# Block products by Strassen's scheme in place of direct 2x2 products, in the dense stages behind attention

## The chip, the cores and the metric

The kernel runs on one core of one Trainium2 chip. The metric is device time in microseconds of the whole program. The engines are TensorE (PE, with its weight loads PEld), VectorE (DVE), ScalarE (ACT), GpSimd (POOL) and SyncE (SP), which issues nearly all DMAs.

## The reference

One layer of a trunk, sequence 1024, width 1024, 16 heads of 64, MLP width 4096, float32. Cut to what matters:

```python
h = rms_norm(x, norm1_g)
q, k, v, bg, cg, xc = split(h @ w_in)                       # six times 1024 columns
y_attn = chunked_relpos_attention(q, k, v, ...)             # band of 9 chunks of 64
u = cg * xc
conv = conv_b + sum(conv_w[j] * pad(u)[:, j:j + s] for j in range(3))
y_attn = y_attn @ w_attn_proj
y_conv = (bg * conv) @ w_conv_proj
g_attn, g_conv = split(sigmoid(h @ w_gate + b_gate))        # 2048 columns
x = x + (g_attn * y_attn + g_conv * y_conv) @ w_out
h2 = rms_norm(x, norm2_g)
u = square(relu(h2 @ w_up))                                 # 4096 columns
x = x + u @ w_down
```

## The kernel before

Activations lie transposed, features on the 128 partitions and the 1024 positions along the row, in two halves `c` of 512. Every dense product has float32 operands that are split in two numbers: `split` has ScalarE copy the value to the short type fp32r (`hi`, L83) and VectorE subtract (`lo`, L84). A product of one tile of 128 inner rows (a k-tile) is then three matmuls, hi x hi, lo x hi and hi x lo, of a 128x128 weight block on 512 columns, added up in one PSUM bank. `fetch_w` loads a weight tile by DMA (`r_...`), `split_w` splits it (`w_...`). `matmul` issues through `pin`, which ties each matmul to the one before it; so TensorE's order is the order of the code. The order of the other engines is a scheduler's; each engine runs its own in order.

The program has these stages. (1) Attention, one pair of heads after the other, with the next pair's projection woven in; in the last pair's place the first NG = 5 row tiles of the gates are woven in. (2) The gates' row tiles 5 to 15: `gate_stages` and `t_stages`, 48 matmuls a row tile (two halves, eight k-tiles, three matmuls), result to DRAM in `gD`. (3) The conv branch: for each of eight row tiles the products c, x and b, the taps on VectorE, the result split into `yc`. (4) The projection of the conv branch (cp), of attention (ap), each times its gate, then the output projection (out), each eight row tiles of 48 matmuls by `t_layout`. The mean square of the residual comes from `mean_square`, two matmuls, a tensor_scalar and a reciprocal for each half. (5) The MLP in 16 steps: `up(k)` makes 256 rows of the hidden layer, `down(k)` adds their products to `acc` in SBUF, with up one step ahead of down. An evacuation of a PSUM bank (the `ev` functions) is one or more VectorE operations for each half.

```python
                for n, (i, j) in enumerate(((0, 0), (1, 0), (0, 1))):
                    matmul(st[c][:], w[:, i, kt % 4, :], mov[c][:, j, kt, :],
                           kt == 0 and n == 0, kt == ND - 1 and n == 2)
```

The whole of the code that the change touches:

Of the kernel before, what the change touches and what calls it, by code (L numbers as in the profile page):

```python
# [40 lines left out]
def block_kernel(ctx, tc, x, xt, wqkv, wcnv, wgate, wcp, wap, wout, wup, wdown,  # L41
# [105 lines left out]
    def t_layout(*a):  # L147
        load, halves = t_stages(*a)
        load()
        for h in halves:  # L150
            for f in h:
                f()

    def new_act(name):
        return [apool.tile([P, 2, ND, HC], F32R, name=f"{name}{c}", tag="act") for c in range(2)]


    hT = new_act("hT")
# [406 lines left out]
    wpool = ctx.enter_context(tc.tile_pool(name="wpool", bufs=2, side="right"))  # L565
    psx = ctx.enter_context(tc.tile_pool(name="psx", bufs=6, space=PSUM))
    banks = [(psx, "x")] * 3 + [(psmm, "mm")] + [(psx, "x")] * 3 + [(psmm, "mm")]
    for t in range(NG, 16):
        if t == NG + 2:
            wp = (wpool, 7, 2)  # L570
        for f in gate_stages(t):
            f()
    att.close()
    acc = [[None] * 2 for _ in range(ND)]

    with tc.tile_pool(name="bpool", bufs=2) as bpool:

        yc = [bpool.tile([P, 2, ND, HC], F32R, name=f"yc{c}", tag="b") for c in range(2)]
        with tc.tile_pool(name="cv", bufs=1) as cv:
            rb2 = cv.tile([P, S], F32, name="rb2")  # L580
            nc.vector.tensor_tensor(rb2[:], rb[:], rb[:], op=ALU.mult)
            for t in range(ND):
                cs = cv.tile([P, S], F32, name=f"cs{t}", tag="cs")
                u = cv.tile([P, S + 2], F32, name=f"u{t}", tag="u")
                y = cv.tile([P, S], F32, name=f"y{t}", tag="y")

                def ev_c(c, ps):
                    cc = slice(c * HC, (c + 1) * HC)
                    nc.vector.tensor_tensor(cs[:, cc], ps[:], rb2[:, cc], op=ALU.mult)

                def ev_x(c, ps):
                    nc.vector.tensor_tensor(u[:, 2 + c * HC:2 + (c + 1) * HC], ps[:],
                                            cs[:, c * HC:(c + 1) * HC], op=ALU.mult)

                def ev_b(c, ps):
                    yy = y[:, c * HC:(c + 1) * HC]
                    nc.vector.tensor_tensor(yy, ps[:], yy, op=ALU.mult)
                    split(yc[c][:, 0, t, :], yc[c][:, 1, t, :], yy)

                t_layout(wcnv[1, t], hT, ev_c, f"c{t}")  # L600
                nc.gpsimd.memset(u[:, 0:2], 0.0)
                t_layout(wcnv[2, t], hT, ev_x, f"x{t}")
                cw = [sv[:, C_CW + 8 * j + t:C_CW + 8 * j + t + 1] for j in range(3)]
                nc.vector.tensor_scalar(y[:], u[:, 2:], cw[2], sv[:, C_CB + t:C_CB + t + 1],
                                        op0=ALU.mult, op1=ALU.add)
                for j in (1, 0):
                    nc.vector.scalar_tensor_tensor(y[:], u[:, j:j + S], cw[j], y[:],
                                                   op0=ALU.mult, op1=ALU.add)
                nc.vector.tensor_tensor(y[:], y[:], rb[:], op=ALU.mult)
                t_layout(wcnv[0, t], hT, ev_b, f"b{t}")  # L610


        aoT = new_act("aoT")
        with tc.tile_pool(name="mg", bufs=2) as mg:
            for p in range(NH // 2):
                for c in range(2):
                    a = mg.tile([P, HC], F32, name=f"a{p}_{c}", tag="a")
                    nc.sync.dma_start(a[:], aoD[p][c][:])
                    split(aoT[c][:, 0, p, :], aoT[c][:, 1, p, :], a[:])

            def gate_of(t, c):
                g = mg.tile([P, HC], F32, name=f"gl{t}_{c}", tag="gl")
                nc.sync.dma_start(g[:], gD[t][:, c * HC:(c + 1) * HC])
                nc.scalar.activation(g[:], g[:], AF.Sigmoid, bias=sv[:, C_BG + t:C_BG + t + 1])
                return g


            for t in range(ND):
                def ev(c, ps, t=t):
                    g = gate_of(ND + t, c)  # L630
                    nc.vector.tensor_tensor(g[:], ps[:], g[:], op=ALU.mult)
                    nc.sync.dma_start(mcD[t][:, c * HC:(c + 1) * HC], g[:])
                t_layout(wcp[t], yc, ev, f"cp{t}")


            mT = [bpool.tile([P, 2, ND, HC], F32R, name=f"mT{c}", tag="b") for c in range(2)]
            for t in range(ND):
                def ev(c, ps, t=t):
                    g = gate_of(t, c)
                    mc = mg.tile([P, HC], F32, name=f"mc{t}_{c}", tag="mc")  # L640
                    nc.sync.dma_start(mc[:], mcD[t][:, c * HC:(c + 1) * HC])
                    nc.vector.tensor_tensor(g[:], ps[:], g[:], op=ALU.mult)
                    nc.vector.tensor_tensor(g[:], g[:], mc[:], op=ALU.add)
                    split(mT[c][:, 0, t, :], mT[c][:, 1, t, :], g[:])
                t_layout(wap[t], aoT, ev, f"ap{t}")


        h2T = new_act("h2T")
        apl = ctx.enter_context(tc.tile_pool(name="apl", bufs=1, side="right"))
        rb2 = rb  # L650
        ssq = [apl.tile([P, HC], F32, name=f"ssq{c}") for c in range(2)]
        for t in range(ND):
            def ev(c, ps, t=t):
                a = acc[t][c] = apl.tile([P, HC], F32, name=f"acc{t}_{c}")
                nc.sync.dma_start(a.rearrange("p (s q) -> p s q", s=4),
                                    xt[4 * c:4 * c + 4, :, t, :].rearrange("s p q -> p s q"))
                nc.vector.tensor_tensor(a[:], ps[:], a[:], op=ALU.add)
                g2 = sv[:, C_G2 + t:C_G2 + t + 1]
                hi = h2T[c][:, 0, t, :]
                nc.scalar.activation(hi, a[:], AF.Copy, scale=g2)  # L660
                nc.vector.scalar_tensor_tensor(h2T[c][:, 1, t, :], a[:], g2, hi.bitcast(F32),
                                               op0=ALU.mult, op1=ALU.subtract)
# [120 lines left out]
```

## Time and profile before

| | us |
|---|---|
| median of 3 runs (1910.21 to 1910.93) | 1910.83 |
| the profiled execution, its own time | 1911.13 |
| its span, first to last instruction | 1909.3 |
| VectorE busy | 1058.8 (55%) |
| ScalarE busy | 560.7 (29%) |
| GpSimd busy | 164.0 (9%) |
| DMA queue 1, share of 16 engines | 28.7% |

The span is what the profile covers; the execution's own time is 1.8 us more. Busy shares are averages over stages. GpSimd's work lies almost all in attention; DMA moves 71 GB/s of HBM traffic on average.

### The profile page before, as it was taken

What the parts mean: (1) busy time and instruction counts of PE and PEld (TensorE: products, weight loads), DVE (VectorE), ACT (ScalarE), POOL (GpSimd) and SP (SyncE); (2) the same over time, 40 slices, a digit from 0 to 9 for tenths busy, and PEclk for the clock granted to TensorE, in tenths of its full rate; (3) what the DMA queues carried; (4) which work ended last, traced back from release to release, by engine and by line L of the source; (5) the groups of instructions that cost most, each with busy time, mean ns of one, the idle gap of its engine ahead of it and who ended that gap; (6) DMA issues with size and microseconds to landing.
All of it is one profiled execution on the core that took longest, in us unless ns stands there. A gap on an engine that the chain in (4) does not pass through costs nothing.

```text
span 1909.3 us, 24631 instructions
## 1 busy us (share of the span) xinstructions
PE 1882.7 (99%) x9268; PEld 1614.8 (85%) x9268; DVE 1058.8 (55%) x1966; ACT 560.7 (29%) x1117; POOL 164.0 (9%) x467
## 2 busy tenths in 40 slices
PE   6899999999999999999999999999999999999999
PEld 6899999999888888888888888888888888888887
DVE  6677877787642234435433445655555555555555
ACT  5455555555431111111232333211111111111110
POOL 5433233233000000000000000000000000000000
PEclk9999999999999999999999999999999999999999
DMA  6443443443322211111364451111111111111112
GB/s 245 111 109 92 104 110 92 111 110 88 111 86 96 94 56 50 50 45 51 109 215 143 144 156 54 36 53 50 50 45 49 52 45 50 50 45 44 50 51 93
DMA packets 91031, 162.08 MB, mean 85 GB/s; under 512 B 10912, under 2 KB 19104, under 8 KB 90912
## 3 DMA queue, kind: packets, MB, share of 16 engines
q1 hardware_dynamic: 90768, 160.48, 28.7%
q8 instruction: 73, 1.20, 0.3%
q14 instruction: 46, 0.38, 0.1%
q10 hardware_dynamic: 144, 0.03, 0.0%
HBM read 114.33 MB, written 20.97 MB: 71 GB/s over the span
## 4 chain that ended last, share of the span: by engine, by line
PE 95%; POOL 2%; DMA 1%; DVE 1%; ACT 1%; issue 0%; SPq 0%; DVEq 0%; POOLq 0%; ACTq 0%
PE ps_u L76 18%; PE pd L76 18%; PE psq L76 12%; PE ps_g L76 9%; PE ps_x L76 5%; PE ps_cp L76 5%; PE ps_o L76 5%; PE ps_ap L76 5%; PE ps_b L76 5%; PE ps_c L76 5%; PE av L76 3%; PE s L76 3%; PE tp L79 3%; POOL qw L115 0%; PE tq L79 0%
## 5 line engine op out<-in xcount | busy, mean ns | idle before, releaser
L76 PE MATMUL psq<-w_q,hT 128*128 128x384 f32 x1536 | 347.9, 352 | 11.2 <-ACT w_q L83 7.6
L76 PE MATMUL ps_u<-h2T,w_u 128*128 128x512 f32 x1536 | 355.2, 392 | 0.0
L76 PE MATMUL pd<-ut,w_d 128*128 128x512 f32 x1536 | 354.0, 391 | 0.0
L76 PEld LDWEIGHTS ps_u<-h2T,w_u 128*128 128x128 f32 x1536 | 288.5, 188 | 63.9 <-issue 1.0
L76 PEld LDWEIGHTS pd<-ut,w_d 128*128 128x128 f32 x1536 | 288.4, 188 | 63.1
L76 PEld LDWEIGHTS psq<-w_q,hT 128*128 128x128 f32 x1536 | 261.7, 193 | 15.2 <-ACT w_q L83 7.6
L719 DVE TENSOR_TENSOR acc<-pd,acc 128x512 f32<-128x512 f32 x256 | 176.5, 690 | 109.9 <-PE pd L76 107.7
L76 PE MATMUL ps_g<-hT,w_g 128*128 128x512 f32 x768 | 187.9, 395 | 0.0
L76 PEld LDWEIGHTS ps_g<-hT,w_g 128*128 128x128 f32 x768 | 140.6, 188 | 27.2
L689 DVE SCALAR_TENSOR_TENSOR rq<-ps_u,rb 128x512 f32<-128x512 f32 x64 | 44.2, 691 | 135.6 <-PE ps_u L76 135.5
L364 ACT ACTIVATE p<-p,sm 128x640 f32<-128x640 f32 (+4 forms) x128 | 89.7, 701 | 80.9 <-DVE sm L362 80.7
L83 ACT CAST ut<-rq 128x512 fp32r<-128x512 f32 x64 | 39.8, 622 | 216.1 <-DVE rq L691 216.1
L83 ACT CAST w_u<-r_u 128x512 fp32r<-128x512 f32 x64 | 39.9, 624 | 185.3 <-PE pd L76 107.7
L362 DVE CUSTOM_DVE_ANT_0 p<-s,b 128x640 f32<-128x640 f32 (+4 forms) x128 | 83.4, 652 | 12.8 <-PE s L76 9.6
L84 DVE TENSOR_TENSOR pt<-tp,pt 128x512 fp32r<-128x512 f32 (+1 forms) x144 | 84.2, 597 | 11.0 <-ACT pt L83 10.4
L76 PE MATMUL ps_x<-hT,w_x 128*128 128x512 f32 x384 | 89.2, 391 | 0.0
L76 PE MATMUL ps_c<-hT,w_c 128*128 128x512 f32 x384 | 89.2, 391 | 0.0
L76 PE MATMUL ps_b<-hT,w_b 128*128 128x512 f32 x384 | 89.2, 391 | 0.0
L76 PE MATMUL s<-k,q 128*128 128x384 f32 (+3 forms) x384 | 82.0, 322 | 6.4 <-DVE sm L362 6.2
L76 PEld LDWEIGHTS av<-pt,vt 128*128 128x128 f32 x576 | 85.5, 188 | 3.1 <-DVE pt L84 1.2
L83 ACT CAST w_d<-r_d 128x512 fp32r<-128x512 f32 x64 | 39.9, 623 | 164.2 <-PE pd L76 142.9
L76 PE MATMUL ps_cp<-yc,w_cp 128*128 128x512 f32 x384 | 88.1, 391 | 0.0
(116 smaller groups left out, 2232.0 us busy)
## 6 DMA issues: line engine op xcount, KB each, us to landing
q<-qh SPq DMA_DIRECT2D x128, 128.0 KB, 2.3
r_u<-in_wup_dram SPq DMA_DIRECT2D x64, 256.0 KB, 2.6
r_d<-in_wdown_dram SPq DMA_DIRECT2D x64, 256.0 KB, 2.7
r_q<-in_wqkv_dram SPq DMA_DIRECT2D x32, 384.0 KB, 3.5
k<-kh SPq DMA_DIRECT2D x64, 128.0 KB, 2.3
r_g<-in_wgate_dram SPq DMA_DIRECT2D x32, 256.0 KB, 2.7
gD<-gp SPq DMA_DIRECT2D x32, 256.0 KB, 2.0
gl<-gD SPq DMA_DIRECT2D x32, 256.0 KB, 2.9
```

Source lines behind the costliest of these rows:

```text
L76: pin(nc.tensor.matmul(ps, lhsT, rhs, start=start, stop=stop))
L79: pin(nc.tensor.transpose(o, i, ident[:]))
L83: return (nc.scalar.copy(hi, src), nc.vector.tensor_tensor(lo, src, hi.bitcast(F32), op=ALU.subtract))
L84: nc.vector.tensor_tensor(lo, src, hi.bitcast(F32), op=ALU.subtract))
L362: nc.vector.tensor_tensor_reduce(pw, sc[:, k0:k1], biast[p, h][:, 5 * P - w:], -1.0, 3e38, ALU.add, ALU.min, sm[:, 0:1])
L364: nc.scalar.activation(pw, pw, AF.Exp, bias=sm[:, 0:1], scale=-1.0, accum_out=sm[:, 1:2])
L689: nc.vector.scalar_tensor_tensor(q[:], ps[:], 0.0, rb2[:, cc], op0=ALU.max, op1=ALU.mult)
L719: nc.vector.tensor_tensor(a[:], ps[:], a[:], op=ALU.add)
```

## The change

Behind attention (and one more gate row tile, t = 5, which stays as it was) all dense products are made in units of 256 output rows by 1024 inner rows by 1024 columns, each by Strassen's scheme in Winograd's form: the unit is cut in 2x2 blocks on each side, and seven block products take the place of eight. There are 61 such units: five for the gates, 12 for conv, four each for cp, ap and out, 16 for up, 16 for down.

The operands are built by other engines. `weights` loads four blocks of weights, makes four sums on GpSimd (L645), and splits seven blocks (L81 on ScalarE, L82 on VectorE). `slot(j, ...)` builds the moving operand for a pair of k-tiles: two loads of 512 KB, four differences on GpSimd (L616), seven splits, in a tile `o[j]` of 7 x 2 x 512. There are four such tiles, and only four: two pools of two (`js`), so that the next phase's `o[j]` takes the place of this phase's.

A phase is a run of units with the same moving operand: gates with conv, cp, ap, out, up, and four quarters of down. The first and the last unit of a phase are `wide`: j outermost, seven PSUM banks, one for each block, and all sums in the evacuation. The others are narrow: block by block, some sums made by adding up in a PSUM bank, three banks. In the last unit of a phase, behind each quarter j, `between(j)` builds the next phase's `o[j]`. So that it can be loaded again, what a phase makes goes through DRAM (`yD`, `mD`, `h2D`, `uD`, beside `aoD` from attention). The MLP is no longer interleaved: 16 units of up, then down in four quarters of 1024 inner rows. The mean square (`ms`) is worked out behind up, and is applied to `acc` at the end, with `x2D` added.

Cut to its core:

```diff
+    def slot(j, name, fetch):
+        b = []
+        for r in range(2):
+            src = bw.stg(f"b{name}{j}_{r}")
+            fetch(src[:], 2 * j + r)
+            b.append([src[:, cols(c)] for c in range(2)])
+        o = js[j // 2].tile([P, 7, 2, HC], F32R, name=f"o{name}{j}", tag="js")
...
+        def minus(i, x, y):
+            t = bw.tt(f"t{name}{j}_{i}")
+            nc.gpsimd.tensor_tensor(t[:], x, y, op=ALU.subtract)
+            put(i, t[:])
+            return t[:]
+        put(0, b[0][0])
+        t1 = minus(3, b[0][1], b[0][0])
+        put(1, b[1][0])
+        t2 = minus(4, b[1][1], t1)
+        put(2, b[1][1])
+        minus(5, b[1][1], b[0][1])
+        minus(6, b[1][0], t2)
+        return o
...
+    def weights(src, name):
+        a = {}
+        for n, k in enumerate(("a11", "a12", "a21", "a22")):
+            a[k] = fetch_w(src[n], [4, P], f"{name}_{k}")
+        w = {i: split_w(a[PROD[i][0]], f"{name}_{i}") for i in (1, 2)}
+        for k, x, y, op in (("s1", "a21", "a22", ALU.add), ("s2", "s1", "a11", ALU.subtract),
+                            ("s3", "a11", "a21", ALU.subtract), ("s4", "a12", "s2", ALU.subtract)):
...
+            nc.gpsimd.tensor_tensor(a[k][:], a[x][:], a[y][:], op=op)
+        for i in ORDER[2:]:
+            w[i] = split_w(a[PROD[i][0]], f"{name}_{i}")
+        return w
+
+    def mms(ps, w, o, i, j, start, stop, chain):
+        x = o[j]
+        for n, (u, v) in enumerate(((0, 0), (1, 0), (0, 1))):
+            matmul(ps[:], w[i][:, u, j, :], x[:, PROD[i][1], v, :], start and n == 0,
+                   stop and n == 2, chain)
...
+    def product(src, o, name, ev, wide=False, between=None):
+        w = weights(src, name)
+        if not wide:
...
+        ps = {}
+        for j in range(4):
+            for i in ORDER:
+                if j == 0:
+                    ps[i] = bank(f"p{i}_{name}")
+                mms(ps[i], w, o, i, j, j == 0, j == 3, False)
+            if between and j < 3:
+                between(j)
+        s1 = snap(ps[1], f"s1_{name}")
+        u2, u4 = etile(f"u2_{name}"), etile(f"u4_{name}")
+        nc.vector.tensor_tensor(u2[:], ps[6][:], s1[:], op=ALU.add)
...
+        nc.vector.tensor_tensor(u4[:], ps[5][:], u2[:], op=ALU.add)
+        nc.vector.tensor_tensor(u2[:], ps[7][:], u2[:], op=ALU.add)
...
+        if between:
+            between(3)
...
+    for k in range(4):
+        nxt = (lambda j, k=k: slot(j, f"u{k + 1}", from_dram(uD, 8 * k + 8))) if k < 3 else None
+        uo = phase([down_job(k, i) for i in range(4)], uo, nxt)
```

The order of the blocks is 1, 2, 6, 7, 5, 4, 3. Blocks 1, 2 and 4 use weights as loaded, the others the four sums.

VectorE where cp ends and ap begins. Names: `gl` holds a gated result, `w_ap0_1` is the second half of the weights of ap's row tile 0. Before:

```order
L631 TENSOR_TENSOR gl13_0_9763<-ps_cp5_0_9738,gl13_0_9763 128x512
L84 TENSOR_TENSOR w_ap0_1_9947<-r_ap0_1_9945,w_ap0_1_9947 128x512
L631 TENSOR_TENSOR gl13_1_9793<-ps_cp5_1_9768,gl13_1_9793 128x512
L84 TENSOR_TENSOR w_ap1_0_10020<-r_ap1_0_10018,w_ap1_0_10020 128x512
L631 TENSOR_TENSOR gl14_0_9833<-ps_cp6_0_9808,gl14_0_9833 128x512
L84 TENSOR_TENSOR w_ap1_1_10025<-r_ap1_1_10023,w_ap1_1_10025 128x512
L631 TENSOR_TENSOR gl14_1_9863<-ps_cp6_1_9838,gl14_1_9863 128x512
```

The same place now. `oa3` is ap's operand slot 3, `ba`/`ta` its loads and differences, `u2`, `u5`, `s1`, `u4` sums of cp's last unit, `w_ap0_2` the weights of block 2 of ap's first unit:

```order
L726 TENSOR_TENSOR u2_cp3_10380<-p7_cp3_10218,u2_cp3_10380 128x512
L729 TENSOR_TENSOR u5_cp3_10391<-p7_cp3_10218,u4_cp3_10381 128x512
L761 TENSOR_TENSOR u2_cp3_10380<-p4_cp3_10226,u2_cp3_10380 128x512
L761 TENSOR_TENSOR u4_cp3_10381<-p3_cp3_10230,u4_cp3_10381 128x512
L82 TENSOR_TENSOR oa3_10414<-ta3_3_10417,oa3_10414 128x512
L82 TENSOR_TENSOR oa3_10414<-ba3_1_10412,oa3_10414 128x512
L82 TENSOR_TENSOR oa3_10414<-ta3_4_10423,oa3_10414 128x512
L82 TENSOR_TENSOR oa3_10414<-ba3_1_10412,oa3_10414 128x512
L82 TENSOR_TENSOR oa3_10414<-ta3_5_10429,oa3_10414 128x512
L82 TENSOR_TENSOR oa3_10414<-ta3_6_10433,oa3_10414 128x512
L82 TENSOR_TENSOR w_ap0_2_10448<-r_ap0_a12_10439,w_ap0_2_10448 128x512
L82 TENSOR_TENSOR w_ap0_6_10457<-ap0_s2_10453,w_ap0_6_10457 128x512
```

Before, next weights and evacuations alternated. Now the lo of the second weight block follows the last unit's sums and the whole of slot 3; ahead of these rows stand slots 0, 1 and 2 with seven lo each, and `w_ap0_1`.

VectorE at the mean square. Before, in the first step of up (`rq` and `ut` evacuate up's first banks):

```order
L676 TENSOR_SCALAR rb_82<-ss2_0_11214 128x512
L677 RECIPROCAL rb_82<-rb_82 128x512
L689 SCALAR_TENSOR_TENSOR rq0_0_0_11230<-ps_u0_0_0_11201,rb_82 128x512
L691 TENSOR_TENSOR rq0_0_0_11230<-ps_u0_0_0_11201,rq0_0_0_11230 128x512
L84 TENSOR_TENSOR ut0_11180<-rq0_0_0_11230,ut0_11180 128x512
L676 TENSOR_SCALAR rb_82<-ss2_1_11248 128x512
L677 RECIPROCAL rb_82<-rb_82 128x512
```

Now, where up ends and down begins (`ou03` is down's slot 3, `w_d0_0_2` a weight block of its first unit):

```order
L82 TENSOR_TENSOR ou03_14355<-tu03_5_14370,ou03_14355 128x512
L82 TENSOR_TENSOR ou03_14355<-tu03_6_14374,ou03_14355 128x512
L946 TENSOR_SCALAR rb_79<-ss2_0_14378 128x512
L946 TENSOR_SCALAR rb_79<-ss2_1_14384 128x512
L948 TENSOR_TENSOR rb_79<-rb_79,sp_11212 128x512 x4
L949 RECIPROCAL rb_79<-rb_79 128x512 x2
L82 TENSOR_TENSOR w_d0_0_2_14417<-r_d0_0_a12_14408,w_d0_0_2_14417 128x512
L82 TENSOR_TENSOR w_d0_0_6_14426<-d0_0_s2_14422,w_d0_0_6_14426 128x512
```

The mean square's eight operations have moved between down's slot 3 and the second weight block of down's first unit.

## Rows read from the trace of the kernel before

**Rows 1.** The page's first line, busy time by engine, and the slices of TensorE.
```profile
span 1909.3 us, 24631 instructions
...
PE 1882.7 (99%) x9268; PEld 1614.8 (85%) x9268; DVE 1058.8 (55%) x1966; ACT 560.7 (29%) x1117; POOL 164.0 (9%) x467
...
PE   6899999999999999999999999999999999999999
...
PEclk9999999999999999999999999999999999999999
```

**Rows 2.** Chain of waits in order of time: start us, us, engine, tile, line, count.
```profile
673.28 10.99 PE ps_c L76 x48
...
936.96 87.89 PE ps_cp L76 x384
1024.86 87.89 PE ps_ap L76 x384
1112.75 87.89 PE ps_o L76 x384
...
1861.60 43.97 PE pd L76 x192
```

**Rows 3.** Windows by stage: busy us of each engine, granted clock, DMA share.
```profile
40.00:50.00 10.00, 6.97 (x26) 6.46 (x27) 6.32 (x10) 5.55 (x10) 7.98 (x16) 0.66 0.45 134
551.22:673.30 122.08, 122.08 (x536) 100.34 (x535) 31.61 (x47) 15.24 (x25) 0.00 (x0) 1.00 0.32 104
673.30:936.96 263.66, 263.66 (x1153) 216.32 (x1153) 114.08 (x144) 39.26 (x63) 0.81 (x8) 1.00 0.17 49
936.96:1024.86 87.90, 87.90 (x386) 72.12 (x385) 32.54 (x49) 31.77 (x50) 0.00 (x0) 1.00 0.62 198
1024.86:1200.64 175.78, 175.78 (x769) 144.22 (x769) 84.67 (x124) 58.49 (x94) 0.00 (x0) 1.00 0.40 117
...
1246.35:1905.60 659.25, 659.20 (x2880) 540.49 (x2879) 361.68 (x541) 106.59 (x171) 0.00 (x0) 1.00 0.17 51
```

**Rows 4.** Groups of ScalarE by shape.
```profile
L83 ACT CAST w_u<-r_u 128x512 fp32r<-128x512 f32 x64 | 39.9, 624 | 185.3 <-PE pd L76 107.7 <-PE ps_u L76 64.8 <-PE ps_o L76 10.8
```

**Rows 5.** Groups of VectorE by shape.
```profile
L84 DVE TENSOR_TENSOR w_u<-r_u,w_u 128x512 fp32r<-128x512 f32 x64 | 44.3, 693 | 13.0 <-ACT w_u L83 11.7
...
L607 DVE SCALAR_TENSOR_TENSOR y<-u,sv,y 128x1024 f32<-128x1024 f32 x16 | 20.6, 1285 | 1.1
...
L677 DVE RECIPROCAL rb<-rb 128x512 f32<-128x512 f32 x2 | 6.7, 3354 | 0.1
...
L676 DVE TENSOR_SCALAR rb<-ss 128x512 f32<-128x512 f32 x2 | 1.4, 688 | 0.8 <-PE ss L76 0.8
```

**Rows 6.** Groups of GpSimd by shape.
```profile
L265 POOL TENSOR_SCALAR qw<-qw,rr 128x4 f32<-128x4 f32 x64 | 21.6, 338 | 221.2 <-DVE qw L263 202.4 <-DVE sm L366 18.2
...
L117 POOL TENSOR_TENSOR qw<-qw 128x4 f32<-128x4 f32 x64 | 13.3, 208 | 5.0
L268 POOL TENSOR_TENSOR qw<-qw 128x4 f32<-128x4 f32 x64 | 13.2, 207 | 5.3
...
L601 POOL MEMSET u<- 128x2 f32 x8 | 0.8, 102 | 422.2 <-DVE y L607 220.9 <-DMA gD<-gp 201.3
...
masks.py:197 POOL MEMSET ident<- 128x128 f32 x1 | 0.2, 205 | 0.3 <-POOLq L771 0.3
```

**Rows 7.** Timeline of VectorE, then GpSimd, 37 to 46 us.
```profile
37.55 0.95 DVE L84 TENSOR_TENSOR w_q<-r_q,w_q 128x768 fp32r<-128x768 f32 x1
38.41 1.22 DVE L190 TENSOR_TENSOR xt<-xt,sv 128x1024 f32<-128x1024 f32 x1
...
42.59 1.22 DVE L190 TENSOR_TENSOR xt<-xt,sv 128x1024 f32<-128x1024 f32 x1
43.73 2.42 DVE L84 TENSOR_TENSOR hT<-xt,hT 128x1024 fp32r<-128x1024 f32 x2
...
37.74 1.95 POOL L265 TENSOR_SCALAR qw<-qw,rr 128x4 f32<-128x4 f32 x1 [0.89 <-DVE qw L263]
...
42.79 2.21 POOL L265 TENSOR_SCALAR qw<-qw,rr 128x4 f32<-128x4 f32 x1 [0.89 <-DVE qw L263]
```

**Rows 8.** DMA issues: count, KB each, median us to landing.
```profile
xn<-in_x_dram SPq DMA_DIRECT2D x8, 512.0 KB, 4.3
...
out_dram<-acc SPq DMA_DIRECT2D x16, 256.0 KB, 2.0
```

**Rows 9.** Timeline of TensorE in attention's first 55 us.
```profile
14.93 12.76 PE L76 MATMUL psq<-w_q,hT 128*128 128x384 f32 x72 [0.60 <-DVE hT L84]
...
42.41 0.47 PE L79 MATMUL tq<-ident,qn 128*128 128x128 f32 x1 [4.08 <-DVE qn L279]
...
45.00 9.94 PE L76 MATMUL psq<-w_q,hT 128*128 128x384 f32 x46 [0.62 <-DVE hT L84]
```

More of the change, by code (lines that the diff above doesn't have):

```diff
@@ L145, in t_stages @@
         return load, [[mm(c, kt) for kt in range(ND)] for c in range(2)]
[L147 to L158, printed above, removed]
+    hpool = ExitStack()
+    apool = hpool.enter_context(tc.tile_pool(name="apool", bufs=2))
+    hT = [apool.tile([P, 2, ND, HC], F32R, name=f"hT{c}", tag="act") for c in range(2)]
     rr = const.tile([P, 2, NT], F32, name="rr")
     rb = const.tile([P, S], F32, name="rb")
+    psm = ExitStack()
+    psmm = psm.enter_context(tc.tile_pool(name="psmm", bufs=2, space=PSUM))
+    banks = [(psmm, "mm")] * 2
     att = ExitStack()
@@ L564, in block_kernel @@
     attp.close()
[L565 to L572, printed above, removed]
-    att.close()
[L574 to L654, printed above, removed]
-                nc.sync.dma_start(a.rearrange("p (s q) -> p s q", s=4),
[L656 to L662, printed above, removed]
@@ new lines, in block_kernel, with __init__, total, times @@
+    class Put:
+        sums = False
+        def __init__(self, put):
+            self.put = put
+    class Add:
+        sums = True
+        def __init__(self, add):
+            self.add = add
+    def total(ps, e):
+        if ps is None or e is None:
+            return ps or e
+        nc.vector.tensor_tensor(e[:], ps[:], e[:], op=ALU.add)
+        return e
+    def times(out, ps, e, x):
+        v = total(ps, e)
+        (nc.vector if v is ps else nc.gpsimd).tensor_tensor(out, v[:], x, op=ALU.mult)
@@ new lines, in value, with phase, build @@
+    def value(out, ps, e):
+        if ps is None or e is None:
+            nc.scalar.copy(out, (ps or e)[:])
+        else:
+            nc.vector.tensor_tensor(out, ps[:], e[:], op=ALU.add)
+    def phase(jobs, o, nxt):
+        made = [None] * 4
+        def build(j):
+            if nxt:
+                made[j] = nxt(j)
+        for n, (src, name, ev) in enumerate(jobs):
+            first, end = n == 0, n == len(jobs) - 1
+            product(src, o, name, ev, first or end, build if end else None)
+        return made
@@ new lines, in block_kernel, with gate_of @@
+    jobs = [gate_job(3)] + sum([conv_jobs(i) for i in range(4)], [])
+    jobs += [gate_job(i) for i in range(4, 8)]
+    yo = phase(jobs, ho, lambda j: slot(j, "y", from_dram(yD)))
+    cvs.close()
+    bw.stack.close()
+    bw = Work("bwb", 4, 3, 4)
+    xws = ExitStack()
+    xw = xws.enter_context(tc.tile_pool(name="xw", bufs=1))
+    def gate_of(t, c):
+        g = xw.tile([P, HC], F32, name=f"gl{t}_{c}", tag="gl", bufs=4)
+        nc.sync.dma_start(g[:], gD[t][:, cols(c)])
+        nc.scalar.activation(g[:], g[:], AF.Sigmoid, bias=sv[:, C_BG + t:C_BG + t + 1])
+        return g
@@ new lines, in cp_job, with put, ap_job @@
+    def cp_job(i):
+        def put(r, c, ps, e):
+            t = 2 * i + r
+            g = gate_of(ND + t, c)
+            times(g[:], ps, e, g[:])
+            nc.sync.dma_start(mcD[t][:, cols(c)], g[:])
+        return wcp[i], f"cp{i}", Put(put)
+    ao = phase([cp_job(i) for i in range(4)], yo, lambda j: slot(j, "a", from_dram(aoD)))
+    def ap_job(i):
+        def put(r, c, ps, e):
+            t = 2 * i + r
+            g = gate_of(t, c)
+            mc = xw.tile([P, HC], F32, name=f"mc{t}_{c}", tag="mc", bufs=2)
+            nc.sync.dma_start(mc[:], mcD[t][:, cols(c)])
+            times(g[:], ps, e, g[:])
+            nc.vector.tensor_tensor(g[:], g[:], mc[:], op=ALU.add)
+            nc.sync.dma_start(mD[t][:, cols(c)], g[:])
+        return wap[i], f"ap{i}", Put(put)
@@ new lines, in block_kernel, with out_job, block, add @@
+    mo = phase([ap_job(i) for i in range(4)], ao, lambda j: slot(j, "m", from_dram(mD)))
+    ssq = xw.tile([P, S], F32, name="ssq")
+    sp = xw.tile([P, S], F32, name="sp")
+    nc.vector.tensor_scalar(sp[:], rb[:], 1.0, None, op0=ALU.add)
+    nc.vector.reciprocal(sp[:], sp[:])
+    nc.vector.tensor_tensor(sp[:], sp[:], rb[:], op=ALU.mult)
+    def out_job(i):
+        blocks = {}
+        def block(r, c):
+            if (r, c) not in blocks:
+                t = 2 * i + r
+                a = blocks[r, c] = xw.tile([P, HC], F32, name=f"x{t}_{c}", tag="gl", bufs=4)
+                nc.sync.dma_start(a.rearrange("p (s q) -> p s q", s=4),
+                                  xt[4 * c:4 * c + 4, :, t, :].rearrange("s p q -> p s q"))
+            return blocks[r, c]
+        def add(r, c, x, first, end):
+            t, a = 2 * i + r, block(r, c)
+            nc.vector.tensor_tensor(a[:], x[:], a[:], op=ALU.add)
+            if end:
+                nc.sync.dma_start(x2D[t][:, cols(c)], a[:])
+                h = etile(f"h{t}_{c}")
+                nc.vector.scalar_tensor_tensor(h[:], a[:], sv[:, C_G2 + t:C_G2 + t + 1],
+                                               sp[:, cols(c)], op0=ALU.mult, op1=ALU.mult)
+                nc.sync.dma_start(h2D[t][:, cols(c)], h[:])
@@ new lines, in add, with up_job, put @@
+                    nc.gpsimd.tensor_tensor(ssq[:, cols(c)], ssq[:, cols(c)], sq[:], op=ALU.add)
+        return wout[i], f"o{i}", Add(add)
+    h2o = phase([out_job(i) for i in range(4)], mo, lambda j: slot(j, "n", from_dram(h2D)))
+    def up_job(i):
+        def put(r, c, ps, e):
+            t = 2 * i + r
+            e = total(ps, e)
+            if e is ps:
+                e = snap(ps, f"ur{t}_{c}")
+            nc.vector.scalar_tensor_tensor(e[:], e[:], 0.0, e[:], op0=ALU.max, op1=ALU.mult)
+            nc.sync.dma_start(uD[t][:, cols(c)], e[:])
+        return wup[i], f"u{i}", Put(put)
@@ new lines, in block_kernel @@
+    uo = phase([up_job(i) for i in range(16)], h2o, lambda j: slot(j, "u0", from_dram(uD)))
+    ms = rb
+    for c in range(2):
+        ps = bank(f"ss2_{c}")
+        matmul(ps[:], ones[:], ssq[:, cols(c)], True, True)
+        m = ms[:, cols(c)]
+        nc.vector.tensor_scalar(m, ps[:], 1.0 / D, EPS, op0=ALU.mult, op1=ALU.add)
+        for _ in range(2):
+            nc.vector.tensor_tensor(m, m, sp[:, cols(c)], op=ALU.mult)
+        nc.vector.reciprocal(m, m)
+    xws.close()
+    bw.stack.close()
@@ new lines, in block_kernel, with down_job, add @@
+    bw = Work("bwc", 2, 2, 2)
+    accp = ctx.enter_context(tc.tile_pool(name="accp", bufs=1))
+    acc = [accp.tile([P, S], F32, name=f"acc{t}") for t in range(ND)]
+    def down_job(k, i):
+        def add(r, c, x, first, end):
+            t = 2 * i + r
+            a = acc[t][:, cols(c)]
+            if k == 0 and first:
+                nc.scalar.copy(a, x[:])
+            else:
+                nc.vector.tensor_tensor(a, x[:], a, op=ALU.add)
+            if k == 3 and end:
+                x2 = etile(f"xr{t}_{c}")
+                nc.sync.dma_start(x2[:], x2D[t][:, cols(c)])
+                nc.vector.tensor_tensor(a, a, ms[:, cols(c)], op=ALU.mult)
+                nc.vector.tensor_tensor(a, a, x2[:], op=ALU.add)
+                nc.sync.dma_start(out[t * P:(t + 1) * P, cols(c)], a)
+        return wdown[k, i], f"d{k}_{i}", Add(add)
```

247 lines of the change are left out of this document (173 added, 74 removed).

## The prediction

> **What bounds the kernel now.** I read the page first: TensorE is busy 99% of the span, at full clock in every slice [rows 1]. Then the chain of waits: from 551 us on it is one unbroken run of matmuls [rows 2]. Its 48 matmuls in 10.99 us are 0.2289 us each; 384 of a projection take 87.89. The windows by stage say the same, with TensorE idle only 0.05 us behind 551 us [rows 3]. So behind attention the time is the number of matmuls times 0.2289 us, and the helpers have slack: VectorE is busy 362 us of 659 in the MLP, GpSimd not at all. Last I read what the helpers' operations cost one by one, because the change hands them work.
>
> **What is taken away.** 16 gate row tiles less the six that stay direct are five products of 256 rows; with conv's 12, cp, ap and out 4 each, up 16 and down 16 that is 61. Each product has 84 matmuls for 96. 61 x 12 = 732 matmuls, at 0.2289 us **167.6 us**. A product then takes 84 x 0.2289 = 19.23 us, a quarter of a wide one (21 matmuls) 4.81, one block's share of a quarter (three) 0.69.
>
> **Products inside a phase.** A product needs seven hi casts on ScalarE (0.62 us [rows 4]) and seven lo subtractions on VectorE (0.69 us [rows 5]), where the direct form had four (two row tiles of two halves). The narrow `up` adds seven operations of evacuation: 14 x 0.69 = 9.7 us of VectorE in 19.23. Conv's triple has 21 lo, 11 sums and four 128x1024 operations of 1.29 us [rows 5], 27 us in 57.7. The weights run a product ahead. I cost these at nothing; TensorE's own time hides them.
>
> **GpSimd's new price.** The trace has no 128x512 operation of two inputs on GpSimd. Nearest rows: a 128x4 tensor_tensor 0.21 us, memset 128x2 0.10 and 128x128 0.21 [rows 6], a slope of 0.82 ns an element, 0.42 us for 512. With one to two such passes on the 0.21 that is 0.63 to 1.05 us; VectorE's row of that shape is 0.69. I take the upper end, 1.1, since a write alone has that slope and two inputs must be read as well. Four a product is 4.4 us of 19.23, hidden.
>
> **Phase changes.** Here the cover ends. There are exactly four operand slots `o[j]`, so the next phase's slot j may be written only when quarter j of the phase's last product (start W, end W+19.23) is done: the first at W+4.81. From there VectorE owes 28 lo for four slots, 7 to 11 evacuation operations and the next weights' lo, and the instruction order puts nearly all of the first two ahead of the second weight. From cp to ap 36 rows stand ahead of `w_ap0_2`: 28 lo, seven sums, `w_ap0_1`. With its own, 37 x 0.69 = 25.5 us, ready at W+30.3; TensorE, which has block 1 done, wants it at W+19.92. That is a **stall of 10.4 us** from VectorE's work alone. The other six weights follow at 0.69 us, TensorE's pace. Before, the weights of ap stood among cp's sums one by one, several tiles early.
>
> By the same count: gates to cp 10, ap to out 9, out to up 10 (36 rows). Up to down has 11 evacuation operations, and the moved mean square as well: two tensor_scalar and four products (0.69), two reciprocals of 3.35 us [rows 5]. 28 + 11 + 1 + 6 = 46 x 0.69 + 6.7 + 0.69 = 39.1; W+43.9 - 19.92 = 24. Before, the same reciprocals stood behind TensorE's matmuls of `up` and held nobody. Each of the three changes between quarters of down has 27 lo and 11 adds ahead even of the first weight: 39 x 0.69 = 26.9, W+31.7 - 19.23 = 12.5. Sum: 10.4 + 10 + 9 + 10 + 24 + 37.5 = **101 us**.
>
> **What comes on top.** (a) Slots 1 to 3 need 12 GpSimd subtractions per change. In the trace a GpSimd operation of 0.34 us on average [rows 6] took 1.95 and 2.21 us when it began beside VectorE operations with two SBUF inputs, and ended as those ended: 37.74 + 1.95 = 39.69, the VectorE run 37.55 to 39.63; 42.79 + 2.21 = 45.00, the first two of the next run ending about 44.9 [rows 7]. The two engines take turns. The lo subtractions have two SBUF inputs, so a subtraction waits for them, and they wait for its result. Full turn-taking is 12 x 1.1 = 13.2 us a change, none if GpSimd finds VectorE's gaps. The row is nearer to turn-taking, but the sums out of PSUM leave gaps: half, 6.6, x 8 = **53 us** (0 to 106).
> The Trainium skill has the rule for this ("SBUF — State Buffer", section on the two separate sides): the pair of ports that VectorE and GpSimd share is an exclusive lock for the whole instruction, also for a VectorE operation with two SBUF inputs, and the loser fully blocks. The trace agrees for GpSimd as the loser; VectorE as the loser is not shown in it, the operations there being too short. By the rule the term would be the upper end, 106. "GPSIMD Engine Reference" (section 3.1) puts two-input elementwise work at 2.6 cycles an element at 1.2 GHz, for 512 elements 1.1 us, an estimate; the sum would be the same.
>
> (b) The start. The gate product that follows attention directly covers 48 x 0.2289 = 11 us. Slots 2 and 3 take the space of `hT`, so they begin behind it: 14 lo = 9.7 us, and `w_g3_3`, seventh block of the first pass, comes after them: 9.7 + 0.69 - 6 x 0.69 = 6 us at least. The whole build is 28 lo, eight 128x1024 operations and 7 weights, 34.4 us, against 11 + 4 us of cover: 19 at most. **12**, since half of it can begin under the direct product.
> (c) After each phase's first product of down, its evacuation and the next weights share VectorE; about 3.5 us (five operations) late for each quarter if none finds room, 0 if all do: **8** of 14.
> (d) The end. Before, one add and one DMA followed the last matmul (1905.57 to 1909.3). The last product is wide, its evacuation 19 operations of which about four run under its last blocks: 15 x 0.69 + 2.0 for the store [rows 8] = 12.4 for 3.7: **8.7**.
> (e) TensorE's clock. After an idle time of 4.08 us the window 40 to 50 us shows 0.66 of the clock [rows 3, 9]: the 46 matmuls then take 9.94 us, against 0.177 each in a run of 72 [rows 9], 8.15, a loss of 1.8. All nine stalls are longer than 4.08 us: **16** (0 to 25, the upper end if the first pass is slow as well).
> DMA is no term: a slot's two loads of 512 KB are 4.3 us (the row of that size [rows 8]) and run a slot ahead.
>
> **Sum.** Against the profiled execution's own 1911.1 us (span 1909.3; the median of the runs is 1910.8, 0.02% away): - 167.6 + 101 + 53 + 12 + 8 + 8.7 + 16 = +31, **1942 us**. I expect no gain: the eight changes of phase hand back what the eighth block saved.
>
> **Rivals.**
> *Faster: VectorE's work is all there is.* GpSimd's subtractions fit the gaps (a = 0), start 7, c 4, clock 8: 1911.1 - 167.6 + 101 + 7 + 4 + 8.7 + 8 = **1872**. For it: casts on ScalarE leave VectorE short pauses, and the sums read PSUM. Against: the 1.95 us row, where GpSimd waited through two operations. It turns at a GpSimd cost of about 4.5 us a change (12 operations of 0.37 us).
> *Full turn-taking.* a = 106, start 19, clock 25, c 14: 1911.1 - 167.6 + 101 + 106 + 19 + 14 + 8.7 + 25 = **2017**. For it: all 12 operations read SBUF on both sides, and VectorE's queue is in order. Against: 7 to 11 of its operations in a change read PSUM.
> *The stalls are not there*, the gain less the end: 1911.1 - 167.6 + 8.7 = **1752**. It would need the weights' lo ahead of the slots' lo, and the order shows them behind.
> *No change*: GpSimd at about 2 us a change, or a few terms smaller, lands at 1911 by chance; nothing holds it there.
>
> **How the numbers follow.** Main case 0.52 (its own range 1915 to 1985), faster rival 0.24, full turn-taking 0.16, no stalls 0.03, no change 0.05. Within 0.2% of 1911 (3.8 us, what a measurement of this kernel can tell from no change) 0.06; faster 0.27, slower 0.67. The range leaves out the no-stall case and half of full turn-taking: 1862 to 2008, from the faster rival less 10 to a little short of the upper one.
>
> **What the profile after would show.** Right: 5124 matmuls of 128x512 behind attention at 0.229 us each; in the chain of waits, VectorE lo of weights (L82) ahead of each phase's first product, eight places of 10 to 30 us, the longest before `d0_0`; GpSimd's 128x512 operations at 1.1 us and more, longest inside the phase changes; a clock under 1.0 there. Wrong: TensorE waiting inside a phase; GpSimd at 0.7 us; waits at the changes below 8 us, or on a DMA of `uD` or `h2D` instead of VectorE. The forecast falls above all if lo subtractions and GpSimd's overlap freely, or if VectorE's 36 rows run ahead of W+4.81.

## The result: slower by 9.3%

| | us |
|---|---|
| before, median of the runs beside it | 1910.58 |
| after, median of 4 runs (2086.45 to 2089.31) | 2088.41 |
| after over before, 95% interval | 1.0929 (1.091 to 1.0948) |
| after, span of the profiled execution | 2087.2 |

The direction was the forecast one; the size was not: 1942 us with a range to 2008. The page of the changed kernel, the lines that answer to [rows 1]:

```profile
span 2087.2 us, 25338 instructions
...
PE 1788.7 (86%) x8536; PEld 1504.9 (72%) x8536; DVE 1390.7 (67%) x2200; ACT 813.4 (39%) x1586; POOL 857.4 (41%) x917
...
PE   7899999999659999996858687899999496959586
...
PEclk9999999999869999998979788899999697979888
```

TensorE has 732 matmuls less, as it should (9268 to 8536), but is no longer unbroken: the dips of the slices are the start behind attention, the middle, and four at the end. The windows of single stretches, the answer to [rows 3] (columns as there), show which: first the start, then changes of phase (last matmul of a phase to the end of the next one's first product), then insides of phases.

```profile
552.65:636.12 83.47, 37.10 (x133) 28.03 (x133) 57.02 (x53) 24.60 (x44) 39.22 (x25) 0.69 0.34 100
946.68:987.78 41.10, 23.44 (x85) 18.20 (x85) 35.21 (x38) 18.21 (x31) 24.32 (x16) 0.75 0.38 134
1052.52:1098.30 45.78, 22.29 (x85) 17.30 (x85) 32.76 (x37) 18.22 (x32) 24.02 (x17) 0.74 0.30 97
...
1627.24:1680.80 53.56, 26.32 (x89) 18.66 (x88) 39.51 (x47) 14.43 (x27) 18.54 (x14) 0.68 0.24 83
...
636.12:946.68 310.56, 310.56 (x1345) 252.04 (x1343) 173.16 (x197) 109.67 (x184) 155.50 (x101) 1.00 0.29 93
...
1098.30:1172.36 74.06, 63.25 (x253) 49.85 (x251) 46.18 (x55) 28.25 (x49) 43.85 (x31) 0.91 0.62 210
...
1333.30:1627.24 293.94, 291.57 (x1262) 236.34 (x1261) 163.36 (x224) 98.47 (x173) 104.71 (x70) 1.00 0.36 118
```

A product's matmuls are 84 x 0.2289 = 19.23 us, so the change from cp to ap (second of the changes shown) has lost 45.78 - 19.23 = 26.6 us. With every stretch worked out in that way, against the terms of the prediction:

| where | lost, us | forecast, us |
|---|---|---|
| start (132 matmuls in 83.5 us) | 53 | 12 and 2 of clock |
| eight changes of phase: 21.9, 26.6, 25.2, 25.7, 34.3, 25.1, 29.4, 25.8 | 214 | 101 + 53 and 14 of clock |
| inside the phases: conv and gates 3, cp 7, ap 16, out 14, up 5, down 22 | 67 | 8 |
| the end (16.1 us behind the last matmul for 3.7) | 12 | 9 |
| sum | 346 | 199 |
| matmuls saved | -167.6 | -167.6 |

346 - 168 = 178 is the difference of the spans. The list of TensorE's waits says who was late (who waited, for whom: us, times, longest):

```profile
PE p_d L74 <- DVE w_d L82: 83.2, 10, 21.5
PE p_ap L74 <- DVE w_ap L82: 17.5, 4, 10.1
PE ps_g L74 <- ACT w_g L81: 17.2, 1, 17.2
PE p_g L74 <- ACT w_g L81: 13.9, 1, 13.9
PE ps_g L74 <- DVE w_g L82: 12.1, 1, 12.1
```

All five wait for a weight's split, as forecast; a load ends none of them directly. In the change from cp to ap TensorE waits three times:

```profile
1060.97 0.80 PE L74 MATMUL p_ap<-oa,w_ap 128*128 128x512 f32 x1 [8.46 <-ACT w_ap L81]
1066.69 1.65 PE L74 MATMUL p_ap<-oa,w_ap 128*128 128x512 f32 x3 [4.92 <-DVE w_ap L82]
1078.45 20.00 PE L74 MATMUL p_ap<-oa,w_ap 128*128 128x512 f32 x80 [10.11 <-DVE w_ap L82]
```

So block 1 was late too, which the prediction took as done at W+19.92: its hi stands in ScalarE's queue behind the slots' casts, which wait for GpSimd's differences, and its lo in VectorE's. The last wait, for block 2, ends the change. What VectorE does meanwhile stands in the timeline of the change from cp to ap (`oa`: ap's operand slots; VectorE's rows first, then GpSimd's):

```profile
1051.24 0.68 DVE L82 TENSOR_TENSOR oa<-ba,oa 128x512 fp32r<-128x512 f32 x1
1051.84 1.76 DVE L82 TENSOR_TENSOR oa<-ta,oa 128x512 fp32r<-128x512 f32 x1
1053.53 0.68 DVE L82 TENSOR_TENSOR oa<-ba,oa 128x512 fp32r<-128x512 f32 x1
1054.13 2.35 DVE L82 TENSOR_TENSOR oa<-ta,oa 128x512 fp32r<-128x512 f32 x2
...
1051.40 1.66 POOL L616 TENSOR_TENSOR ta<-ba 128x512 f32<-128x512 f32 x1 [0.63 <-DVE oa L82]
1053.74 1.59 POOL L616 TENSOR_TENSOR ta<-ba,ta 128x512 f32<-128x512 f32 x1 [0.68 <-DVE oa L82]
```

A lo subtraction takes 0.68 us where GpSimd has nothing, and 1.76 where GpSimd has started first: 1.08 us of GpSimd's operation, then its own 0.68. GpSimd's 1.66 is the same the other way: it waits for the subtraction that is running and then needs about 1.1. So where a lo subtraction and a difference meet, the engines take full turns, and GpSimd's price of 1.1 was right. From 1052.5 us, where TensorE ran dry, to 1078.45 VectorE has no gap: 28 operations in 25.95 us, 0.93 each for the forecast 0.69. Then TensorE gets `w_ap0_2`: W, the start of cp's last product, is 1033.15, so at W+45.3; full turns by the prediction were 30.3 + 13.2 = 43.5. The sums out of PSUM are not slowed (VectorE's two rows, then GpSimd's, which runs beside them):

```profile
1066.56 0.68 DVE L761 TENSOR_TENSOR s_cp<-p_cp,s_cp 128x512 f32<-128x512 f32 x1
1067.16 0.67 DVE L725 TENSOR_TENSOR u_cp<-p_cp,u_cp 128x512 f32<-128x512 f32 x1
...
1066.06 1.73 POOL L616 TENSOR_TENSOR ta<-ba,ta 128x512 f32<-128x512 f32 x1
```

But they begin at 1064.89 us, and this is the last of the change's differences.

### The profile page after: what moved, and what is told of

It reads as the page before. It is cut to its first block, busy times and chain, and to the rows that moved or that the text cites. A ratio compares the mean times of both kernels' runs of the same rounds, so it can differ in the third digit from the quotient of the medians.

```text
span 2087.2 us, 25338 instructions
## 1 busy us (share of the span) xinstructions
PE 1788.7 (86%) x8536; PEld 1504.9 (72%) x8536; DVE 1390.7 (67%) x2200; ACT 813.4 (39%) x1586; POOL 857.4 (41%) x917
## 5 line engine op out<-in xcount | busy, mean ns | idle before, releaser
L74 PE MATMUL p_d<-ou,w_d 128*128 128x512 f32 x672 | 172.3, 416 | 89.6 <-DVE w_d L82 83.2
L74 PEld LDWEIGHTS p_d<-ou,w_d 128*128 128x128 f32 x672 | 132.7, 200 | 129.7 <-DVE w_d L82 92.4
L74 PE MATMUL pa_u<-on,w_u 128*128 128x512 f32 x672 | 162.7, 394 | 2.4 <-DVE s_u L761 1.9
L74 PEld LDWEIGHTS pa_u<-on,w_u 128*128 128x128 f32 x672 | 126.0, 188 | 32.3 <-DVE s_u L761 2.4
L74 PE MATMUL pa_d<-ou,w_d 128*128 128x512 f32 x384 | 98.8, 410 | 11.9 <-DVE acc L964 11.9
L74 PE MATMUL ps_g<-hT,w_g 128*128 128x512 f32 x288 | 80.9, 411 | 29.3 <-ACT w_g L81 17.2
L82 DVE TENSOR_TENSOR w_u<-r_u_a,w_u 128x512 fp32r<-128x512 f32 x80 | 64.2, 804 | 51.5 <-ACT w_u L81 51.2
L74 PEld LDWEIGHTS pa_d<-ou,w_d 128*128 128x128 f32 x384 | 75.4, 197 | 30.6 <-issue 13.1
L82 DVE TENSOR_TENSOR pt<-tp,pt 128x512 fp32r<-128x512 f32 (+1 forms) x144 | 84.1, 596 | 11.6 <-ACT pt L81 11.0
L81 ACT CAST pt<-tp 128x512 fp32r<-128x512 f32 (+1 forms) x144 | 71.8, 516 | 41.4 <-PE tp L77 41.2
L645 POOL TENSOR_TENSOR u_s<-r_u_a,r_u_a 128x512 f32<-128x512 f32 x16 | 22.5, 1407 | 158.5 <-DMA r_u_a<-in_wup_dram 150.5
L74 PE MATMUL av<-pt,vt 128*128 128x256 f32 (+1 forms) x576 | 86.7, 272 | 0.9 <-DVE pt L82 0.9
L81 ACT CAST w_d<-r_d_a 128x512 fp32r<-128x512 f32 x80 | 49.0, 621 | 96.6 <-PE pb_d L74 29.4
L74 PE MATMUL pb_u<-on,w_u 128*128 128x512 f32 x336 | 82.2, 394 | 0.0
L82 DVE TENSOR_TENSOR w_d<-r_d_a,w_d 128x512 fp32r<-128x512 f32 x80 | 65.5, 827 | 23.6 <-ACT w_d L81 23.3
```

The costliest lines, as they stand in the source:

```text
L74: pin(nc.tensor.matmul(ps, lhsT, rhs, start=start, stop=stop, skip_group_check=chain))
L81: return (nc.scalar.copy(hi, src), nc.vector.tensor_tensor(lo, src, hi.bitcast(F32), op=ALU.subtract))
L82: nc.vector.tensor_tensor(lo, src, hi.bitcast(F32), op=ALU.subtract))
L645: nc.gpsimd.tensor_tensor(a[k][:], a[x][:], a[y][:], op=op)
```

## Experiments

Theory 1: in a change of phase VectorE and GpSimd work in turns, and the sum of both stands ahead of the weights. Theory 2: VectorE's own queue sets it, GpSimd runs beside it. Theory 3: the operands' loads through DRAM and the few staging buffers set it.

**no_differences**

```diff
-            t = bw.tt(f"t{name}{j}_{i}")
-            nc.gpsimd.tensor_tensor(t[:], x, y, op=ALU.subtract)
-            put(i, t[:])
-            return t[:]
+            put(i, x)
+            return x
```

> Leaves out the four GpSimd differences of each operand slot: the undiminished block is split in their place, so the operands of four of the seven blocks are not the ones of the scheme. Theory 1 (VectorE and GpSimd take turns, 1.07 us for each GpSimd operation on top of each 0.68 us subtraction): the eight changes of phase lose 12 to 16 operations each, 13 to 17 us, and the start some 10 to 15; in all 115 to 150 us less than the changed kernel, that is 1940 to 1975. Theory 2 (VectorE's own queue alone sets the changes, GpSimd runs beside it): 0 to 15 us less. Theory 3 (loads of the operands through DRAM and the few staging buffers set them): under 10 us less.

1980.1 us (ratio 1.0377, 1.0357 to 1.0398): 108 less than the changed kernel. Theory 2 and 3 allowed 15 and 10. Theory 1's span was 115 to 150, a little missed: 144 operations at 108 us are 0.75 us for each, against a turn of 1.07. The sum of the table, made from this run's trace, says where: the eight changes lose 131 us for 214, the start 33 for 53, the insides 61 for 67. So part of the turns in the changes cost nothing; ap's first four differences, for one, ran 70 us ahead of its change. The run also takes away ScalarE's waiting for the differences; the next one leaves that in place.

**differences_on_vector**

```diff
-            nc.gpsimd.tensor_tensor(t[:], x, y, op=ALU.subtract)
+            nc.vector.tensor_tensor(t[:], x, y, op=ALU.subtract)
```

> The slots' four differences are made by VectorE instead of GpSimd, nothing else. Theory 1: each costs VectorE 0.69 us in place of a turn of 1.07, so about 0.4 us less for each of 12 to 16 operations in eight changes and the start, 40 to 55 us less, 2035 to 2050. Theory 2: VectorE has 0.69 us more for each of 128 operations, 60 to 90 us more, 2150 to 2180. Theory 3: within 10 us of the changed kernel's 2088.

2033.9 us (1.0646, 1.063 to 1.0662): 54 less, at theory 1's upper end. More work for VectorE, the engine that is waited for, made the kernel faster, which rules theory 2 out. All loads are as before, so theory 3 (within 10 us) is out as the main cause. Its timeline in the same change, where lo and differences (L616) run at 0.68 alike:

```profile
1030.99 0.69 DVE L82 TENSOR_TENSOR oa<-ta,oa 128x512 fp32r<-128x512 f32 x1
1031.59 0.68 DVE L82 TENSOR_TENSOR oa<-ba,oa 128x512 fp32r<-128x512 f32 x1
1032.19 0.68 DVE L616 TENSOR_TENSOR ta<-ba,ba 128x512 f32<-128x512 f32 x1
1032.79 0.68 DVE L616 TENSOR_TENSOR ta<-ba,ta 128x512 f32<-128x512 f32 x1
```

**mean_square_early**

```diff
+            if i == 8 and (r, c) == (0, 0):
+                mean_square()
...
-    ms = rb
-    for c in range(2):
-        ps = bank(f"ss2_{c}")
```

> The eight VectorE operations of the mean square (with two reciprocals of 3.35 us) and its two matmuls move from behind up to its ninth product. Theory 1 and 2 alike: they stood in VectorE's queue ahead of the second weight of down, so 10 to 13 us less, 2075 to 2078. If another thing was late there (the last operand slot's loads): within 4 us of 2088.

2077.5 us (1.0874, 1.0857 to 1.089): 11 less, as both theories of a queue had it. Of the 34 us of the change from up to down, 11 are this move (23.8 are left by its trace); six operations of 0.69 us and two of 3.35 are 10.8.

**gate_first**

```diff
-    for j in range(2):
-        ho[j] = slot(j, "h", fetch_h)
     gp = (bw.pool, "e", bw.n[0])
     for f in gate_stages(NG):
         f()
+    for j in range(2):
+        ho[j] = slot(j, "h", fetch_h)
```

> At the start the direct gate product's code stands ahead of operand slots 0 and 1, so its weights are split before them. Theory 1: VectorE and GpSimd have the same work to do (four slots of about 11.7 us each with turns, and seven weights), and it still ends late, so TensorE's two waits of 17.2 and 12.1 us go, but the wait ahead of the first Strassen product grows; 5 to 15 us less in all. If the order alone made the loss: the 29 us of the two waits go, 2059.

2082.5 us (1.0903, 1.0887 to 1.0919): 6 less. The waits of 17.2 and 12.1 us ahead of the direct gate product have become one of 6.5, and that ahead of the first Strassen product has grown to

```profile
PE p_g L74 <- DVE w_g L82: 37.6, 1, 37.6
```

The start loses 49 us for 53 by its trace: it is bound by the work of building, too, and the order mostly moves the place of the wait.

**one_operand**

```diff
-            if nxt:
-                made[j] = nxt(j)
+            made[j] = ho[j]
```

> Every phase uses the operand slots that were built at the start; no slots are built later, so all products behind the first phase have the wrong moving operand. All else stays: weights, evacuations, writes to DRAM. It prices the building of slots in the eight changes of phase, whose excess over 84 matmuls each is 22 to 34 us in the changed kernel, 226 us in all. If the building is the cause (theory 1): 190 to 230 us less, 1860 to 1900. If the rest of a change (seven PSUM banks emptied at once, the next weights late) costs half of it: 1960 or more.

1923.0 us (1.007, 1.0053 to 1.0087): 165 less, for 190 to 230. The eight changes lose 58 us for 214 and the insides 55 for 67 by the same sum, so building the slots is some three quarters of the changes, not all. (The slots' loads go with them, so this run alone does not part theory 1 from theory 3; the first two do.) What is left waits for weights still, 12.5 us where the mean square stands, 8.2 at up, 2 to 4 at the others, and inside phases for evacuations:

```profile
PE p_d L74 <- DVE w_d L82: 21.6, 4, 12.5
...
PE pa_d L74 <- DVE acc L963: 12.0, 3, 6.6
PE p_u L74 <- DVE w_u L82: 8.9, 2, 8.2
...
PE pa_ap L74 <- ACT u_ap L658: 7.5, 1, 7.5
PE pa_o L74 <- DVE x L909: 7.4, 1, 7.4
```

Even with no slot built behind the first phase this form is no faster than before, because start, insides and end alone cost 120 us of the 168 saved.

**sums_on_vector**: differences_on_vector, mean_square_early and gate_first together, and the sums of the weights moved as well.

```diff
-            nc.gpsimd.tensor_tensor(a[k][:], a[x][:], a[y][:], op=op)
+            nc.vector.tensor_tensor(a[k][:], a[x][:], a[y][:], op=op)
```

> The slots' differences and the four sums of the weights on VectorE, the mean square behind the ninth product of up, and the direct gate product ahead of the slots: GpSimd is left with the products of the evacuations. Theory 1: 2088 - 54 - 11 - 6, and 1.5 us less for the sums of the weights in each of eight changes, 2003 to 2017: still slower than before, since VectorE's own work of a change (28 lo, 16 differences, 7 to 11 sums, weights) is longer than the 14.4 us that cover it. If GpSimd was the only trouble: at or under 1911.

2011.4 us (1.0531, 1.0515 to 1.0547), inside the span. With hardly a turn left it is still 101 us slower than before, and by its trace the eight changes still lose 164 us: VectorE's own work in a change is longer than its cover.

**up_only**: the form to which the runs point. The saving of 12 matmuls for each product has to pay for a moving operand that is built once for a phase: 16 products pay 44 us for one build (up), four pay 11 (cp, ap, out, a quarter of down), less than the 22 us of the cheapest change. So the kernel before, with the scheme in up alone. Down loads its operand `ut` from DRAM 256 rows at a time, ahead. Its core:

```diff
+        if t in (1, 3):
+            o[t // 2] = slot(t // 2, hs[t - 1:t + 1])
+    w_u0 = weights(wup[0], "u0")
...
+    for j in range(2, 4):
+        o[j] = slot(j, hs[2 * j:2 * j + 2])
...
+        product(wup[i], o, f"u{i}", Put(put), i == 0, w=w_u0 if i == 0 else None)
+        if i == 4:
+            mean_square()
+        if i == 9:
+            load_u(0, uta)
```

> The kernel before with Strassen's scheme in up alone: 16 products with one moving operand. Slots 0 and 1 are built under the direct output projection, from the tiles in SBUF, slots 2 and 3 behind its end; all differences and sums on VectorE; the weights of the first product ahead of slots 2 and 3; up writes to DRAM, and down stays direct and loads its operand 256 rows at a time, ahead. 16 x 12 x 0.2289 = 44 us less work. Slots 2 and 3 are 22 VectorE operations of 0.65 us, 14.3 us and some 4 us of chain, against 9.6 us of cover: 5 to 10 us lost. By theory 1 and 2 alike 1872 to 1882, faster than before; if a product of Strassen's scheme has a loss of its own inside a phase (2 us or more for each), 1900 or more.

1868.05 us (0.9778, 0.9763 to 0.9793): 42.6 us faster than before, the best of all runs, and 4 us better than the span: the 5 to 10 us of late slots are not there. Three things beside the number of products differ from the changed kernel's slots: they come from tiles in SBUF, VectorE does all the operations, and the first weights stand ahead of slots 2 and 3. Only the second was varied alone (the next run). The timeline of TensorE across the end of out (`p_u` is up's first product) has no wait but one of 1 us:

```profile
1189.68 9.00 PE L77 MATMUL ps_o<-mT,w_o 128*128 128x512 f32 x39
1198.52 19.36 PE L77 MATMUL p_u<-on,w_u 128*128 128x512 f32 x84
1217.72 2.94 PE L77 MATMUL pa_u<-on,w_u 128*128 128x512 f32 x12
1220.50 2.94 PE L77 MATMUL pc_u<-on,w_u 128*128 128x512 f32 x12
1223.27 0.39 PE L77 MATMUL pa_u<-on,w_u 128*128 128x512 f32 x1
1224.72 2.81 PE L77 MATMUL pa_u<-on,w_u 128*128 128x512 f32 x11 [1.06 <-DVE w_u L85]
```

**up_only_gpsimd**: up_only with both sums and differences on GpSimd; the edit is against up_only.

```diff
-            nc.vector.tensor_tensor(t[:], x, y, op=ALU.subtract)
+            nc.gpsimd.tensor_tensor(t[:], x, y, op=ALU.subtract)
...
-            nc.vector.tensor_tensor(a[k][:], a[x][:], a[y][:], op=op)
+            nc.gpsimd.tensor_tensor(a[k][:], a[x][:], a[y][:], op=op)
```

> The kernel up_only with its differences and sums put back on GpSimd, nothing else: the same turn-taking where other work covers it. Theory 1 with cover: inside up VectorE has 14 operations of 0.69 us and gives four turns of 1.07, 14 us of 19.4, so nothing is lost there; the eight differences of slots 2 and 3 take 1.07 for 0.69 and the chain through two engines is longer, 0 to 6 us. So 1868 to 1874. If turns with GpSimd cost TensorE time wherever they are: 61 x 4 turns in the changed kernel, here 16 x 4 of 1.07 us, 1895 or more.

1875.5 us (0.9817, 0.9803 to 0.9831), 7.4 more than up_only and 1.5 above the span. Six waits of 0.2 to 2.4 us, all in the first two products, make 6.7 us of it; the longest:

```profile
PE pa_u L77 <- DVE s_u L839: 2.4, 1, 2.4
PE p_u L77 <- DVE on L85: 1.7, 2, 1.2
PE pa_u L77 <- DVE w_u L85: 1.6, 1, 1.6
```

The other 14 products have the same turns (GpSimd's sums take 1.36 to 1.63 us on average there) and no wait. In these two runs, turns cost only where VectorE has no slack.

## Why the prediction missed

By the table the forecast was 147 us short: 59 inside the phases, 46 in the eight changes, 39 at the start and 3 at the end. **The saving** was right, 732 matmuls. So was the place of most of the loss, the queue of VectorE ahead of the weights, with GpSimd's operation at 1.1 us.

**Inside the phases** lay the largest miss. The step that failed is "I cost these at nothing; TensorE's own time hides them", with (c), 8 us in down, as the only term: 67 came. The rule held for conv, the gates and up (up's 1260 matmuls lose 5 us), not for phases of four products, two of which are wide. TensorE is idle (the windows' length less PE's busy time) for 40 of the 67 us. In out (4.35 and 3.2) and down (2.7, 2.7 and 6.5) the waits are for VectorE, where a wide product's sums and the next weights' lo stand in one queue; down's idle time, 13 us, is within the 14 that (c) set as its upper end. In cp they are for ScalarE's copies of a bank (2.2, 2.3 and 1.2). In ap most of it is one wait, behind transfers, where the prediction had "DMA is no term":

```profile
1131.34 0.72 ACT L861 ACTIVATE gl<-gl,sv 128x512 f32<-128x512 f32 x1 [7.82 <-DMA gl<-gD]
...
1136.71 0.56 ACT L658 COPY u_ap<-pa_ap 128x512 f32<-128x512 f32 x1
...
1137.33 5.49 PE L74 MATMUL pa_ap<-oa,w_ap 128*128 128x512 f32 x12 [8.35 <-ACT u_ap L658]
```

ScalarE's sigmoids of the gates wait for their loads ahead of the copy that TensorE needs. Whether earlier loads or more `gl` buffers would remove this was not tried. The other 27 us are matmuls that run slower: some 8 in the narrow products (see the last section), the rest behind the waits (see the clock).

**Term (a), turn-taking**, failed in its size and its reason: "half, 6.6", because the sums that read PSUM were to leave gaps. They do, but behind the differences, so in the change from cp to ap nearly every turn is paid (the forecast's full turns come out within 2 us). [rows 7] had shown GpSimd waiting through two operations. The Trainium skill's rule ("SBUF — State Buffer", section on the two separate sides), an exclusive lock in which either side may be the loser, is what the rows of this case show, now for VectorE too: 1.76 us for 0.68. Over the eight changes no_differences puts the price at 83 us, for 53 forecast and 106 at full. TensorE's idle time there points the same way: 175 us, for 101 + 53 = 154 and, at full, 207. That 101 + 106 and 14 of clock come to 221, near the 214 measured, is partly luck, since the clock had too little in it. Even the rival with full turns, 2017 us, stays 71 below the measured time.

**Term (b), the start**, was mis-sized: 53 us for 14. It took the direct gate product as cover, and did not see that its weights stand behind slots 0 and 1 in the queues (VectorE comes to them at 581.97 us, 29 us into the start); so there was no cover. It also had no price for GpSimd's 16 differences there, which no_differences puts at 20 us, and none for the first slot's loads, for which VectorE waits 6.15 us in its timeline. gate_first shows that with the cover the start would still have cost some 49.

**Term (e), the clock**, was mis-sized too: 16 us for about 43. In the table it is not apart from the waits, but the windows have it: what PE's busy time is above 0.2289 us a matmul. For cp to ap that is 22.29 - 85 x 0.2289 = 2.8 us; for all eight changes 36 (without the mean square's own matmuls), for the start 7. It is an estimate, rather too high, since the ends of matmuls are modelled. Behind the wait before down's last quarter:

```profile
1979.89 22.50 PE L74 MATMUL p_d<-ou,w_d 128*128 128x512 f32 x83 [21.47 <-DVE w_d L82]
```

The window of its first 13 matmuls (1979.89 to 1986.00) has a granted clock of 0.50, the lower level of 1.2 GHz, that of its last 50 (1991.00 to 2002.20) 1.00: 22.5 us for 83 matmuls that take 19.0 at 0.2289. In ap, behind its wait of 8.35 us, 12 matmuls take 5.49 us instead of 2.77. The prediction took 1.8 us from a wait of 4.08; the waits here are longer.

**The end** cost 12 for 9, since the reload of the residual (`xr`, 2.5 to 4.9 us a transfer in the chain of waits) stands in it too.

## What to carry to other kernels

A scheme that trades TensorE's work for operands that other engines build pays by the number of products that share an operand, and by what covers the build: here 16 for one build, half of it under other work, gained 42.6 us; four for one build lost. Number alone is not enough: in the changed kernel the gates with conv have 17 products for one build, saved 17 x 2.75 = 47 us, and lost 53 + 3 to a start without cover. The scheme there with a covered build was not tried. Cost such a build as one queue: these subtractions of VectorE and GpSimd, with both inputs in SBUF, took turns where they met in the changes, and where VectorE was the one waited for, having GpSimd do the differences made the kernel 54 us slower than having VectorE do them. Read the cover from the engine that must do the building, in its instruction order, and not from TensorE's time.

## What the runs showed of the hardware that was not expected

The matmuls of a narrow product take a little longer at the same granted clock of 1.00: in the timeline of up_only its blocks of 12 follow each other at 2.77 us, 0.231 a matmul, where direct products have 0.2289 (48 in 10.99 [rows 2]). The wide product there does not: its 84 matmuls take from 1198.52 to 1217.72, 0.2286 each, though it changes the bank every three. Over the 43 narrow products of the changed kernel that is 8 us, part of the losses above. The cause was not looked for.
